# Moving a conditional block from the last group of experts to the middle of the expert loop

## The chip, the cores and the metric

The kernel runs on one core of a Trainium2 chip. The core has five engines that run their own instruction streams: PE (TensorE, the matrix engine), DVE (VectorE), ACT (ScalarE), POOL (GpSimd) and SP (SyncE, which here issues nearly all the DMAs). The engines wait for one another through semaphores. The metric is the time of one execution on the device in microseconds; the median of three runs of the kernel before is 983.52 us (981.23 to 983.72).

## The reference

Two decoder layers act on a residual stream of 256 tokens by 1024 channels, in float32. A layer first mixes tokens (differential attention and sparse attention, then an output projection and a layer norm), and then works on channels. The change is in the second part:

```python
def hierarchical_moe(x, w_rg, b_rg, w_re, b_re, w_g, w_u, w_d):
    ...                      # top-1 of 4 groups, then top-2 of 8 experts in it: weights comb
    for g in range(N_GROUPS):
        hg = silu(einsum('nd,edf->nef', xt, w_g[g])) * einsum('nd,edf->nef', xt, w_u[g])
        y = y + einsum('nef,efd->nd', hg * comb[:, g, :, None], w_d[g])
    return y
...
ffn = hierarchical_moe(x, ...)
ple = sigmoid(x @ w_ple_gate[i]) * (p[i] @ w_ple[i])
x = layer_norm(ALPHA * x + ffn + ple, ln2_g[i], ln2_b[i])
```

There are 32 experts, each with gate, up and down matrices (1024x256, 1024x256, 256x1024), so that a layer reads 96 MB of expert weights. A token goes to two of them.

## The kernel before

**Tiling.** The 32 experts are ranked by how many tokens they have. The 12 with the most get 64 slots each, the other 20 get 32 slots. They are worked on in 11 groups of 128 rows: six groups of two experts with 64 rows each, and five of four experts with 32 rows. In the order of the loop (`gi` = 0 to 10) the groups gi = 0, 1, 2, 4, 6 and 8 are of two experts, and gi = 3, 5, 7, 9 and 10 of four. An expert's weights are six loads of 512 KB: four of gate and up, two of down. So a group of two brings 12 loads, a group of four 24.

**A group.** `slots_of` marks and gathers the tokens of a group (PE products with the 0/1 marks `gs`), `front` multiplies the gathered tokens with the gate and up weights and applies the activation (`sil`), and `back` turns `sil` around (line 95, two transposes), copies it to `hT` (line 1058, ACT), multiplies it with the down weights, splits the product in two parts (lines 208 and 209, ACT and DVE) and adds them up into the four accumulators `acc` (`combine`). In the columns of PE's array each expert of a group has its own strip, of 64 or 32 columns; a 128x512 product of 32 columns is written `128*32 128x512` in the rows. Nearly all products go through one helper, line 92. The loop runs ahead by one: `front(gi + 1)` is issued before `back(gi)`.

**The block.** Some expert could have more tokens than slots. Then `rest` (line 1078 and around) works through what is left over, in two loops over experts (lines 1196 and 1198). The whole stands under `tc.If(most > 0)` (line 1195), where `most` is read from a small tensor `cmi` (line 1194) into a register of each engine. In the profiled execution `most` is zero in both layers: the block is jumped over, and the loops never run. On SP the way that skips the block ends in nine semaphore instructions (rows at line 1195), which bring the semaphores of SP's DMAs to the counts that the block would have left.

**Other work in the loop.** At gi = 4, 5 and 6 the pieces of the per-layer embedding (`Embed`, products of `x` and `p` with 256 columns) are worked in. At gi = 9 the two vectors of the layer norm are loaded (`wide`, line 382). At the last group of the first layer four weights of the next layer are loaded ahead (`ahead`, line 164).

**What sets the order.** A scheduler orders each engine's instructions from the program's order and its own estimates; a conditional is a border that it keeps: what the program has after the block is issued after it, with exceptions that the order below shows. Weights live in 47 places of 512 KB (`Held`). A load (`fetch`: line 1032 reads the expert's number, line 1038 issues the DMA; `load`: line 164) needs a free place, and so waits until PE has made the last product with what was there. All weight loads go through SP's one queue, in order: a load that waits holds all behind it. Eight semaphores are used in turn, so that at most eight loads are under way.

Of the kernel before, what the change touches and what calls it, by code (L numbers as in the profile page):

```python
# [23 lines left out]
DEPTH = 2  # L24
# [55 lines left out]

@with_exitstack
def tile_hybrid_trunk(ctx: ExitStack, tc: tile.TileContext, x_in, xT_in, pT_in, pos_in, ws, wik, wrt, lnv,
                      brt, lamv, sublnv, out, places=47, t2b=4, young=4, gsb=1, hTb=1, silb=2, nring=5, early=(4, 5, 6), nahead=4, apart=8, npre=36, wA=1, wB=1, wC=1, wD=1, wE=3, inorder=2, e0=3, e1=3,  nearly_=0, peng_=1, ifat=10, im=0, df=0, dh=15, nol=0, diag=1, rpool='0000', lastemb=1, lastat=6, pre_if=(4,5), npair=6, fh=False, fg=0, order=(0,1,2,6,3,7,4,8,5,9,10), engs=None, nemb=1, nwarm=9, nfine=2, nah=4, o1=False, o2=False, o3=True, o4=True, order2=True, pa=2, pb=7, f1=True):
    nc = tc.nc
    V, A, G = nc.vector, nc.scalar, nc.gpsimd

# [37 lines left out]
    def bank():  # L124
        return ps.tile([P, 512], F32, tag="mm", bufs=4, name=nm("mm"))

    def wt(shape, dt, tag, bufs):
        return wk.tile(shape, dt, tag=tag, bufs=bufs, name=nm(tag))
# [3 lines left out]
    class Held:  # L132
# [11 lines left out]
        def free(self):  # L144
            arena.give(self.b)
# [16 lines left out]
    def load(l, i, shape):  # L162
        r = Held(shape, load=True)
        nc.sync.dma_start(r.t, ws[l, i])
        return r
# [56 lines left out]
    ahead, ready = [], []  # L222
# [156 lines left out]
    def wide(i, l):  # L379

        r = Held([D])
        nc.sync.dma_start(r.v[0:1], lnv[l, i:i + 1])
        G.partition_broadcast(r.v, r.v[0:1])  # L383
        return r
# [68 lines left out]
    for l in range(DEPTH):  # L453
# [3 lines left out]
        ahead, ready = [], []  # L457
# [420 lines left out]
        groups = [[(r, 2, 64)] for r in range(0, 2 * npair, 2)]  # L878
# [9 lines left out]
        if order:  # L888
            groups = [groups[i] for i in order]

        def experts(gi):

            c = 0
            for r, n, w in groups[gi]:
                for i in range(n):
                    yield r + i, slice(c, c + w)
                    c += w

        def gather(gs, xg, halves=(0, 1)):

            for k4 in halves:
                b = bank()
                for k in range(4):
                    ks = slice((4 * k4 + k) * P, (4 * k4 + k + 1) * P)
                    for t in range(TT):
                        PE.matmul(b[:, k * P:(k + 1) * P], x[t].v[:, ks], gs[:, t, :], start=t == 0, stop=t == TT - 1)
                A.activation(xg.half[k4], b.rearrange("p (k s) -> p k s", k=4), AF.Copy)  # L907
# [17 lines left out]
        def marks_of(gi):  # L925

            gs = wt([P, TT, P], F32, "gs", gsb)
            c = 0
            for r, n, w in groups[gi]:
                marked[0] = V.tensor_tensor(gs[:, :, c:c + n * w].rearrange("p t (e s) -> p t e s", e=n),  # L930
                                            iom[:, None, None, :w].to_broadcast([P, TT, n, w]),
                                            posm[:, :, r:r + n, None].to_broadcast([P, TT, n, w]), op=OP.is_equal)
                c += n * w
            return gs

        def ways_of(gi, gs):

            sT = wt([P, TT, P], F32R, "sT", 2)
            bw = ways(gs, [cw[:, :, r:r + n] for r, n, w in groups[gi]], sT)
            wsl = wt([P, 1], F32, "wsl", 3)  # L940
            for i, (r, sl) in enumerate(experts(gi)):
                V.tensor_copy(wsl[sl], bw[sl, i:i + 1])
            return sT, wsl

        def slots_of(gi):
            gs, xg = marks_of(gi), Gathered(gi >= fg)
            gather(gs, xg)
            return xg, *ways_of(gi, gs)

        b = bank()  # L950
        places = bank()
# [61 lines left out]
        def between():  # L1013
            with in_turn():
                gather(gs, first, (1,))
            with in_turn():
                for t in range(TT):
                    PE.matmul(b[:, t * NE:(t + 1) * NE], combT[:, t * P:(t + 1) * P], perm, start=True, stop=True)
            with in_turn():
                r = ways_of(0, gs)  # L1020
            ranked = el4.rearrange("p t g e -> p t (g e)")
            V.tensor_copy(ranked, b[:, :2 * NE].rearrange("p (t e) -> p t e", t=TT))
            V.tensor_scalar(mks, ranked, 0.0, None, op0=OP.is_gt)
            V.tensor_copy(cw[:, :, NFIX:], ranked[:, :, NFIX:])
            return r
# [3 lines left out]
        def fetch(r, j):  # L1029

            if r >= NFIX and r not in ranks:
                ranks[r] = nc.sync.value_load(ids[0:1, r:r + 1], min_val=0, max_val=NE - 1)
            fetched[r, j] = Held([2, 512], load=True)
            if r < NFIX:
                src = ws[l, O_EXP + 6 * r + j]
            else:
                src = ws[l, ds(O_EXP + 6 * ranks[r] + j, 1)].rearrange("o p n -> (o p) n")
            nc.sync.dma_start(fetched[r, j].t, src)

        def weights_of(gi, js):  # L1040
            for j in js:
                for r, _ in experts(gi):
                    if (r, j) not in fetched:
                        fetch(r, j)
            return [[fetched.pop((r, j)) for r, _ in experts(gi)] for j in js]

        def hidden_act(gu, wsl, sil):
            A.activation(sil, gu[:, :FE], AF.Sigmoid)  # L1048
            V.scalar_tensor_tensor(sil, sil, wsl, gu[:, :FE], op0=OP.mult, op1=OP.mult)  # L1049
            V.tensor_tensor(sil, sil, gu[:, FE:], op=OP.mult)  # L1050
            return sil
# [71 lines left out]
        def front(gi, xg, sT, wsl, between=None):  # L1123

            sl = [sl for _, sl in experts(gi)]
            n = len(sl)
            wr = weights_of(gi, range(4))
            gu = bank()
            for kt in range(KT):
                for i in range(n):  # L1130
                    PE.matmul(gu[sl[i], :], xg.half[kt // 4][:, kt % 4, sl[i]],
                              wr[kt // 2][i].v[:, kt % 2, :], start=kt == 0, stop=kt == KT - 1)
                if kt % 2:
                    free(*wr[kt // 2])
                if kt == KT // 2 - 1 and between:
                    sT, wsl = between()
            xg.free()
            return hidden_act(gu, wsl, wt([P, FE], F32, "sil", silb)), sT
# [35 lines left out]
        for gi in range(len(groups)):  # L1174
            if gi == e1:
                emb[0].products(0, range(wE, KT + 2))
                emb[0].gate()
                emb[0].add(0)
            if gi == e0:
                emb[0].run(1)  # L1180
            if gi in early:
                q = 1 + early.index(gi)
                if q not in emb:
                    emb[q] = Embed(q)
                emb[q].run(0)
                if q < 3:
                    emb[q].run(1)
            if gi == ifat:
                for j in pre_if:
                    for r, _ in experts(gi):  # L1190
                        fetch(r, j)
                if l < DEPTH - 1:
                    ahead.extend(load(l + 1, i, [2, 512]) for i in range(nah))
                most = nc.values_load(cmi[0:1, 0:1], min_val=0, max_val=S)
                with tc.If(most > 0):
                    with tc.For_i(0, NBIG, 1) as r:
                        rest(r, 64, 2)
                    with tc.For_i(NBIG, NE, 1) as r:
                        rest(r, 32, 1)
            after = front(gi + 1, *slots_of(gi + 1)) if gi + 1 < len(groups) else None  # L1200
            if gi == lastat and (l == DEPTH - 1 or lastemb == 2):
                emb[3].run(1)
            ys, sT = back(gi, *held), held[1]
            held = after
            if gi == last - 1:
                lng, lnb = wide(2, l), wide(3, l)
                xn = [Held([D]) for _ in range(TT)]
                if l < DEPTH - 1:
                    xT = Split(KT)
# [102 lines left out]
```

## Time and profile before

| | |
|---|---|
| median of three runs | 983.52 us (981.23 to 983.72) |
| profiled execution, its own time | 980.9 us |
| its span in the trace | 978.8 us |
| mean granted clock of TensorE | 0.988 |
| PE busy | 936.4 us, 96% |
| DVE, ACT, POOL busy | 425.9, 348.1, 33.5 us |
| moved by DMA | 280.81 MB, mean 287 GB/s |

The span is the time from the first to the last instruction that the profiler saw. "Busy" counts the time in which an engine executes, without its waits, branches and DMA issues. The two layers lie at 0 to some 480 us and 480 to 978 us; the expert loop takes about the second half of each.

### The profile page before, as it was taken

What the parts mean: (1) busy time and instruction counts of PE and PEld (TensorE: products, weight loads), DVE (VectorE), ACT (ScalarE), POOL (GpSimd) and SP (SyncE); (2) the same over time, 40 slices, a digit from 0 to 9 for tenths busy, and PEclk for the clock granted to TensorE, in tenths of its full rate; (3) what the DMA queues carried; (4) which work ended last, traced back from release to release, by engine and by line L of the source; (5) the groups of instructions that cost most, each with busy time, mean ns of one, the idle gap of its engine ahead of it and who ended that gap; (6) DMA issues with size and microseconds to landing.
All of it is one profiled execution on the core that took longest, in us unless ns stands there. A gap on an engine that the chain in (4) does not pass through costs nothing. (4 is left out here: it accounts for less than half of the span.)

```text
span 978.8 us, 14760 instructions
## 1 busy us (share of the span) xinstructions
PE 936.4 (96%) x5185; PEld 608.9 (62%) x5185; DVE 425.9 (44%) x1066; ACT 348.1 (36%) x704; POOL 33.5 (3%) x36
## 2 busy tenths in 40 slices
PE   8999999999999999999699999999999999999983
PEld 5877777886445665444388767787754555664441
DVE  6796566863121121112468854768621211111113
ACT  6557586522111111111346667765111111111110
POOL 0000000100000000001310000001000000000010
PEclk9999999999999999999799999999999999999997
DMA  8994335777889999993899233466778899999823
GB/s 296 398 415 162 124 108 198 250 267 270 307 322 417 400 407 366 391 415 119 325 415 382 91 127 129 151 215 222 279 279 337 326 419 392 403 362 417 353 68 150
DMA packets 79010, 280.81 MB, mean 287 GB/s; under 512 B 9160, under 2 KB 9928, under 8 KB 78928
## 3 DMA queue, kind: packets, MB, share of 16 engines
q1 hardware_dynamic: 78784, 279.78, 75.2%
q8 instruction: 44, 0.72, 0.3%
q14 instruction: 38, 0.31, 0.1%
q10 hardware_dynamic: 144, 0.00, 0.0%
HBM read 278.70 MB, written 1.05 MB: 286 GB/s over the span
## 5 line engine op out<-in xcount | busy, mean ns | idle before, releaser
L92 PE MATMUL acc<-a,a 128*128 128x512 f32 x1440 | 352.2, 398 | 2.6 <-ACT a L208 1.8
L92 PEld LDWEIGHTS acc<-a,a 128*128 128x128 f32 x1440 | 266.0, 189 | 65.2 <-issue 3.2
L92 PE MATMUL mm<-a,a 128*32 128x512 f32 (+6 forms) x1456 | 240.7, 512 | 0.0
L208 ACT ACTIVATE a<-a 128x512 fp32r<-128x512 f32 (+1 forms) x247 | 150.7, 631 | 99.8 <-PE acc L92 66.5
L209 DVE TENSOR_TENSOR a<-a,a 128x512 fp32r<-128x512 f32 (+1 forms) x239 | 160.6, 692 | 51.5 <-ACT a L208 50.6
L92 PEld LDWEIGHTS mm<-a,a 128*32 128x32 f32 (+4 forms) x1456 | 111.7, 141 | 103.8 <-issue 94.8
L92 PE MATMUL mm<-a,hT 128*32 128x512 f32 (+1 forms) x512 | 113.5, 632 | 6.1 <-ACT hT L1058 5.9
L92 PEld LDWEIGHTS mm<-gs,a 128*128 128x128 f32 x704 | 85.5, 191 | 17.9 <-issue 13.5
L92 PE MATMUL mm<-gs,a 128*128 128x128 f32 x704 | 91.2, 278 | 0.0
L209 DVE TENSOR_TENSOR t<-mm,t 128x512 fp32r<-128x512 f32 x44 | 30.1, 691 | 137.1 <-ACT t L208 137.1
L1049 DVE SCALAR_TENSOR_TENSOR sil<-sil,wsl,mm 128x256 f32<-128x256 f32 x22 | 10.6, 480 | 131.5 <-ACT sil L1048 131.4
L208 ACT ACTIVATE t<-mm 128x512 fp32r<-128x512 f32 x44 | 26.0, 597 | 110.7 <-PE mm L92 109.6
L92 PE MATMUL acc<-t,sT 128*128 128x512 f32 x176 | 60.8, 441 | 2.9 <-ACT t L208 2.9
L92 PEld LDWEIGHTS mm<-a,hT 128*32 128x32 f32 (+1 forms) x512 | 26.9, 123 | 58.8 <-issue 41.9
L1048 ACT ACTIVATE sil<-mm 128x256 f32<-128x256 f32 x22 | 8.5, 384 | 140.2 <-PE mm L92 140.2
L92 PEld LDWEIGHTS acc<-t,sT 128*128 128x128 f32 x176 | 28.5, 189 | 33.8 <-ACT t L208 17.4
L907 ACT ACTIVATE a<-mm 128x512 f32<-128x512 f32 x40 | 23.9, 597 | 66.8 <-PE mm L92 66.7
L920 DVE CAST sT<-mm 128x256 fp32r<-128x256 f32 x22 | 9.3, 425 | 61.2 <-PE mm L92 58.6
L763 DVE TENSOR_TENSOR sil<-sil,mm 128x256 f32<-128x256 f32 x16 | 6.7, 420 | 53.5 <-ACT sil L762 53.5
L548 ACT ACTIVATE t<-mm,mx 128x128 f32<-128x128 f32 (+1 forms) x64 | 26.1, 422 | 10.7 <-DVE mx L545 10.7
L383 POOL PARTITION_BROADCAST a<-a x8 | 10.3, 1314 | 543.4 <-DMA a<-lnv 540.5
L762 ACT ACTIVATE sil<-mm 128x256 f32<-128x256 f32 x16 | 6.1, 384 | 57.9 <-PE mm L92 53.7
(195 smaller groups left out, 649.9 us busy)
## 6 DMA issues: line engine op xcount, KB each, us to landing
a<-ws SPq DMA_DIRECT2D x523, 512.0 KB, 8.6
a<-x_in SPq DMA_DIRECT2D x2, 512.0 KB
out<-a SPq DMA_DIRECT2D x4, 256.0 KB, 2.6
a<-xT_in SPq DMA_DIRECT2D x3, 256.0 KB, 5.6
a<-wik SPq DMA_DIRECT2D x2, 288.0 KB, 8.3
a<-ws SPq DMA_DIRECT2D x2, 256.0 KB, 4.2
pT<-pT_in SPq DMA_DIRECT2D x2, 256.0 KB, 9.3
a<-wrt SPq DMA_DIRECT2D x2, 144.0 KB, 2.5
```

The source lines that it names most:

```text
L92: self.last = nc.tensor.matmul(*a, **k)
L208: copied[0] = A.activation(hi, src, AF.Copy)
L209: copied[1] = eng.tensor_tensor(lo, src, hi, op=OP.subtract)
L383: G.partition_broadcast(r.v, r.v[0:1])
L548: A.activation(e[:, i * nk:(i + 1) * nk], b[:, i * nk:(i + 1) * nk], AF.Exp, bias=mx[:, i:i + 1], accum_out=sums[i])
L762: A.activation(g, b[:, :256], AF.Sigmoid)
L763: V.tensor_tensor(g, g, b[:, 256:], op=OP.mult)
L907: A.activation(xg.half[k4], b.rearrange("p (k s) -> p k s", k=4), AF.Copy)
L920: V.tensor_copy(sT, b[:, :2 * P].rearrange("p (t q) -> p t q", t=TT))
L1048: A.activation(sil, gu[:, :FE], AF.Sigmoid)
L1049: V.scalar_tensor_tensor(sil, sil, wsl, gu[:, :FE], op0=OP.mult, op1=OP.mult)
```

## The change

The condition moves from `gi == 10` to `gi == 3` (the default of `ifat`), and in the loop body from ahead of `front(gi + 1)` to behind it. So the block now stands behind the products of `front(4)`, the fifth group, and ahead of `back(3)`. The early loads of the last group's down weights (`pre_if`) and of the next layer's weights, which stood ahead of the block, go; `back(10)` issues both itself. The reading of `most` stays ahead of `front`.

```diff
-    ... ifat=10, ...
+    ... ifat=3, ...
             if gi == ifat:
-                for j in pre_if:
-                    for r, _ in experts(gi):
-                        fetch(r, j)
-                if l < DEPTH - 1:
-                    ahead.extend(load(l + 1, i, [2, 512]) for i in range(nah))
                 most = nc.values_load(cmi[0:1, 0:1], min_val=0, max_val=S)
+            after = front(gi + 1, *slots_of(gi + 1)) if gi + 1 < len(groups) else None
+            if gi == ifat:
                 with tc.If(most > 0):
                     with tc.For_i(0, NBIG, 1) as r:
                         rest(r, 64, 2)
                     with tc.For_i(NBIG, NE, 1) as r:
                         rest(r, 32, 1)
-            after = front(gi + 1, *slots_of(gi + 1)) if gi + 1 < len(groups) else None
```

Lines behind the change stand four lower afterwards, and the conditional itself at line 1192.

In SP's queue, first layer, this stood before around the new place (a_2803 is the last gate and up load of group gi = 4; a_2826 to a_2840 are the eight down loads of gi = 3; a_2963 to a_3020 the gate and up loads of gi = 5; a_3059 to a_3065 the down loads of gi = 4; L164 with a_3098 to a_3102 the weights of an `Embed`):

```order
L1038 DMA a_2803<-ws 128x1024
L1038 ISA
L1038 DMA a_2826<-ws 128x1024
...
L1038 DMA a_2840<-ws 128x1024
L1032 TENSOR_LOAD ids_2224
L1032 ISA x2
L1038 ISA
L1038 DMA a_2963<-ws 128x1024
...
L1038 DMA a_3065<-ws 128x1024
L164 DMA a_3098<-ws 128x1024
L164 DMA a_3100<-ws 128x1024
L164 DMA a_3102<-ws 128x1024
```

And this stands there now (a_2817 is the last gate and up load of gi = 4, the left-out rows are 19 more readings of line 1032; a_3416 to a_3420 are the same three `Embed` weights as a_3098 to a_3102, and a_3144 is the first down load of gi = 3):

```order
L1038 DMA a_2817<-ws 128x1024
L1032 TENSOR_LOAD ids_2224
L1032 ISA x2
...
L164 DMA a_3416<-ws 128x1024
L164 DMA a_3418<-ws 128x1024
L164 DMA a_3420<-ws 128x1024
L1192 COMPARE_AND_BRANCH
...
L1192 UNCONDITIONAL_BRANCH
L1038 ISA
L1038 DMA a_3144<-ws 128x1024
```

The 28 loads a_2826 to a_3065 moved from ahead of the three `Embed` loads to behind the block, and twenty readings of expert numbers moved ahead of it. Behind the block SP has 126 loads of 512 KB before it comes to the layer norm's vectors at line 382. The three `Embed` loads wait for the same products of PE as they did: the last one for the `128*128 128x256` products of `Embed` that end at about 301.7 us.

On PE, first layer, this stood before behind the products of `front(4)` (mm_2805; mm_2842 is the transposes of `back(3)`, and mm_2847 its down products, in the strips of the four experts, a_2826 to a_2840 being their weights):

```order
L92 MATMUL mm_2805<-a_2803,a_2740 64x512
L95 MATMUL mm_2842<-identr,sil_2669 128x128 x2
L92 MATMUL mm_2847<-a_2826,hT_2845 32x512
L92 MATMUL mm_2847<-a_2828,hT_2845 32x512
L92 MATMUL mm_2847<-a_2830,hT_2845 32x512
L92 MATMUL mm_2847<-a_2832,hT_2845 32x512
L92 MATMUL mm_2847<-a_2834,hT_2845 32x512
L92 MATMUL mm_2847<-a_2836,hT_2845 32x512
```

And this stands there now (mm_3165 and mm_3182 are the two halves of the same down product; mm_3199 is a product of `Embed` over all 128 columns, whose inputs have been there since before):

```order
L1192 UNCONDITIONAL_BRANCH
L95 MATMUL mm_3160<-identr,sil_2669 128x128 x2
L92 MATMUL mm_3165<-a_3144,hT_3163 32x512
L92 MATMUL mm_3182<-a_3144,hT_3163 32x512
L92 MATMUL mm_3165<-a_3146,hT_3163 32x512
L92 MATMUL mm_3182<-a_3146,hT_3163 32x512
L92 MATMUL mm_3199<-a_2308,a_2069 128x256 x4
L92 MATMUL mm_3165<-a_3148,hT_3163 32x512
L92 MATMUL mm_3182<-a_3148,hT_3163 32x512
L92 MATMUL mm_3199<-a_2310,a_2070 128x256 x3
L92 MATMUL mm_3165<-a_3150,hT_3163 32x512
L92 MATMUL mm_3182<-a_3150,hT_3163 32x512
```

Before, eight products of one half stood in a row, with four different strips next to one another. Now the two halves of one weight, in one strip, stand together, and products over all columns stand between them; the other four weights follow in the same manner.

## Rows read from the trace of the kernel before

**Rows 1.** Waits of the tensor engine, whole span: total us, times, longest
```profile
PE mm L95 <- PEq L1195: 13.7, 2, 7.3
PE mm L92 <- ACT hT L1058: 5.9, 11, 0.8
```

**Rows 2.** Timeline, TensorE, end of first layer: start, us, idle before
```profile
462.34 2.16 PE L92 MATMUL acc<-t,sT 128*128 128x512 f32 x8 [0.70 <-ACT t L208]
470.93 0.66 PE L95 MATMUL mm<-identr,sil 128*128 128x128 f32 x2 [6.43 <-PEq L1195]
472.40 6.75 PE L92 MATMUL mm<-a,hT 128*32 128x512 f32 x32 [0.81 <-ACT hT L1058]
```

**Rows 3.** Line 1195, first layer: ns (min, median, max), first and last start
```profile
L1195 SPq EVENT_SEMAPHORE  x9: 17/17/17, 471.2 to 480.7; - x9
...
L1195 PEldq COMPARE_BRANCH  x1: 6359/6359/6359, 464.3 to 464.3; - x1
```

**Rows 4.** Line 1195, second layer
```profile
L1195 PEldq COMPARE_BRANCH  x1: 7379/7379/7379, 951.1 to 951.1; - x1
```

**Rows 5.** Waits of SP's queue, first layer, 436 to 462
```profile
SPq L382 <- PE mm L92: 18.1, 1, 18.1
```

**Rows 6.** The same, second layer, 915 to 948
```profile
SPq L382 <- PE mm L92: 22.9, 1, 22.9
```

**Rows 7.** Line 1038, last down loads, first layer
```profile
L1038 SPq DMA_DIRECT2D a<-ws x8: 333/368/447, 460.8 to 464.7; - x8
...
DMA to landing us min/median/max: 4.6/6.9/8.1
```

**Rows 8.** The same, second layer
```profile
L1038 SPq DMA_DIRECT2D a<-ws x8: 332/369/662, 947.8 to 952.1; - x8
...
DMA to landing us min/median/max: 3.3/5.7/7.3
```

**Rows 9.** Timeline, TensorE, end of second layer
```profile
959.97 5.55 PE L92 MATMUL mm<-a,hT 128*32 128x512 f32 x32 [0.53 <-ACT hT L1058]
```

**Rows 10.** Timeline of SP's queue around the new place, first layer
```profile
265.12 38.14 SPq L1038 DMA_DIRECT2D a<-ws  x31
304.09 2.81 SPq L164 DMA_DIRECT2D a<-ws  x3
```

**Rows 11.** The same, second layer
```profile
786.83 2.81 SPq L164 DMA_DIRECT2D a<-ws  x3
```

**Rows 12.** Line 1032, reads of an expert's number on SP, whole span
```profile
L1032 SPq TENSOR_LOAD <-ids x52: 262/268/461, 227.9 to 891.7; - x52
```

**Rows 13.** Timeline, TensorE, around the new place, first layer
```profile
298.96 2.75 PE L92 MATMUL mm<-a,a 128*128 128x256 f32 x12
307.07 7.09 PE L92 MATMUL mm<-a,a 128*64 128x512 f32 x32
315.00 2.76 PE L92 MATMUL mm<-a,hT 128*32 128x512 f32 x18 [0.47 <-ACT hT L1058]
...
318.37 1.06 PE L92 MATMUL mm<-a,hT 128*32 128x512 f32 x8
...
320.03 1.06 PE L92 MATMUL mm<-a,hT 128*32 128x512 f32 x6
...
335.84 7.07 PE L92 MATMUL mm<-a,a 128*32 128x512 f32 x64
...
348.81 1.07 PE L92 MATMUL mm<-a,hT 128*64 128x512 f32 x2
```

**Rows 14.** Stretches: us, busy of PE, PEld, DVE, ACT, POOL; PEclk, DMA share, GB/s
```profile
321.00:400.00 79.00, 77.55 (x475) 46.95 (x472) 14.22 (x37) 13.20 (x28) 0.00 (x0) 1.00 0.97 385
400.00:438.00 38.00, 37.15 (x217) 18.00 (x220) 6.01 (x16) 5.22 (x10) 0.00 (x0) 1.00 1.03 416
438.00:460.00 22.00, 22.00 (x166) 10.47 (x162) 4.13 (x11) 3.33 (x7) 0.00 (x0) 1.00 0.32 131
...
470.90:479.50 8.60, 7.76 (x36) 2.65 (x37) 0.69 (x1) 1.76 (x4) 1.21 (x1) 0.60 0.94 375
```

More of the change, by code (lines that the diff above doesn't have):

```diff
@@ L82, in tile_hybrid_trunk @@
 def tile_hybrid_trunk(ctx: ExitStack, tc: tile.TileContext, x_in, xT_in, pT_in, pos_in, ws, wik, wrt, lnv,
-                      brt, lamv, sublnv, out, places=47, t2b=4, young=4, gsb=1, hTb=1, silb=2, nring=5, early=(4, 5, 6), nahead=4, apart=8, npre=36, wA=1, wB=1, wC=1, wD=1, wE=3, inorder=2, e0=3, e1=3,  nearly_=0, peng_=1, ifat=10, im=0, df=0, dh=15, nol=0, diag=1, rpool='0000', lastemb=1, lastat=6, pre_if=(4,5), npair=6, fh=False, fg=0, order=(0,1,2,6,3,7,4,8,5,9,10), engs=None, nemb=1, nwarm=9, nfine=2, nah=4, o1=False, o2=False, o3=True, o4=True, order2=True, pa=2, pb=7, f1=True):
+                      brt, lamv, sublnv, out, places=47, t2b=4, young=4, gsb=1, hTb=1, silb=2, nring=5, early=(4, 5, 6), nahead=4, apart=8, npre=36, wA=1, wB=1, wC=1, wD=1, wE=3, inorder=2, e0=3, e1=3,  nearly_=0, peng_=1, ifat=3, im=0, df=0, dh=15, nol=0, diag=1, rpool='0000', lastemb=1, lastat=6, pre_if=(4,5), npair=6, fh=False, fg=0, order=(0,1,2,6,3,7,4,8,5,9,10), engs=None, nemb=1, nwarm=9, nfine=2, nah=4, o1=False, o2=False, o3=True, o4=True, order2=True, pa=2, pb=7, f1=True):
     nc = tc.nc
```

## The prediction

> **What bounds the kernel now.** I read the waits of the tensor engine first. Over the whole span only one wait of PE is large: 13.7 us in two pieces, both at the conditional block; the next cause, copies by ACT, adds up to 5.9 us in 11 pieces of at most 0.8 [rows 1]. No DMA is among its waits. So PE is the bound, and its one gap is what the change moves. Then I looked at where the gap lies. In the first layer PE ends the additions of group 9 at 464.50 (462.34 + 2.16), stands 6.43 us, and does the 32 down products of the last group from 472.40 to 479.15 [rows 2]. The gap is the branch itself: the instruction takes 6.36 us on PE in the first layer [rows 3] and 7.38 in the second [rows 4].
>
> Third, what else was late in that place. SP's queue stood 18.1 us (to 459.96) in the first and 22.9 us (to 946.95) in the second layer, at the layer norm's vectors, waiting for a place that PE had to release [rows 5, 6]; the last group's eight down loads stand behind it. They were issued up to 464.7 and 952.1, and the slowest landed 8.1 and 7.3 us later [rows 7, 8], so by about 472.8 and 959.4. PE's products began 0.4 before the one and 0.6 after the other [rows 2, 9]. So at the end the branch lies beside a transfer that PE would have waited for anyway. That is the first thing to see: the gap is 13.7 us, but what can be won by taking it away is less.
>
> Fourth, the new place. There SP is well ahead of PE. It issues the loads of line 1038 without a break until 303.3, and then the three Embed loads, at 304.09 to 306.90 [rows 10] and from 786.83 in the second layer [rows 11].
>
> **The change part by part.**
>
> *The end.* Without the branch, PE can end the last down products no sooner than the last weight's landing, and what is left then: one weight's two halves in one strip. A piece of two matmuls of this kind takes 1.07 [rows 13], two pieces in a strip some 1.9 (2 x 1.07 less 0.2 that they share, an estimate from these rows). So 474.7 instead of 479.15, and 961.3 instead of 965.52 (959.97 + 5.55): at most 4.4 and 4.2 us. [...] I take 2 per layer, the middle. The early loads that were removed from ahead of the block cost nothing, since these loads keep their place behind line 382.
>
> *PE's branch in the middle.* It stands behind the 32 products of front(4), 7.09 us [rows 13]. Its price has no row in the middle. From above it is 7.38 us [rows 4]. From below it is 0: PE's queue may run ahead of its products, and the branch may be taken while they still run. At the end it could not, because the last additions waited for ACT, and so the branch began at 464.3, 0.2 before they ended [rows 2, 3]. I take 5 us, nearer to the two rows that exist.
>
> [...]
>
> *PE's order behind the block.* Before, back(3) makes its 32 products in pieces of 18, 8 and 6, in 2.76 + 1.06 + 1.06 = 4.9 us [rows 13]: four strips run side by side. Behind the block the two halves of one weight stand together, in one strip, and full-width Embed products between them. The order makes six turns of the eight weights (two of them have two weights side by side, four have one). A turn is 4 matmuls in a strip, some 1.9 us as above; six are 11.4, 6.5 more than before. From above: eight turns, 15.2, so 10.3 more. From below: 0, if the turns overlapped fully. That a piece costs the same however little is in it, the rows show: 8 matmuls take 1.06 and 6 take 1.06, but 2 also take 1.07.
>
> So PE comes out of the middle 5 + 6.5 = 11.5 us later in each layer.
>
> *SP's queue.* The block makes SP wait until all of its loads under way have landed: at the end the nine semaphore instructions began at 471.2 and the last at 480.7 [rows 3]. In the middle it comes to the branch behind the three Embed loads, and the last of these waits for PE's Embed products, which end at 301.71 (298.96 + 2.75) [rows 13]. The 20 readings of expert numbers ahead of it, 0.27 us each and 5.4 in all [rows 12], lie within that wait. From 301.8 on: the last Embed load lands 3.3 us after issue, as into an empty queue [rows 8], so at 305.1; some 0.5 for the semaphores; the first down load lands at 305.6 + 3.3 = 308.9. Its own eight follow at 1.26 us each (524288 bytes at 416 GB/s [rows 14]), the last at 317.7. PE's first down product stands at 315.0 plus the branch; it is hardly held. The next 16, for front(5), have landed by 338, and PE, which began these at 335.84 [rows 13] and now 11.5 later, isn't held either.
>
> But 28 loads are now behind the block that had been issued by 304: some 35 us of transfer. What stood in SP at line 382 is the slack for it. 126 loads lie between the block and line 382. At 1.28 us (between 1.26 and the 1.36 of the 385 GB/s stretch [rows 14]) the last lands at 308.9 + 125 x 1.28 = 468.9, where SP was released at 459.96 before: 8.9 late. In the second layer all this lies 481.8 later (its L164 loads, at 786.83, 482.7), so 790.7 + 160 = 950.7 against 946.95: 3.8 late. Both are under PE's own 11.5, so PE's lateness sets the release, and the stream is beside it. At 1.26 they would be 6.4 and 1.3, at 1.36 18.9 and 13.8 late.
>
> *The sum.* Per layer 5 + 6.5 - 2 = 9.5, for two layers 19. The profiled execution took 980.9 us (span 978.8); 19 more are 999.9. The median of the runs is 2.6 above it, so I predict 983.5 + 19 = 1002.5 us.
>
> **The rivals.**
>
> *The middle covers it, and it gets faster.* If the branch is taken while the products of front(4) run, and the turns overlap, then the middle costs nothing and the end gives 4.4 + 4.2: 983.5 - 8.6 = 974.9. For it: the weights for the next products lie ready, and SP had 18 to 23 us of slack. Against it: 35 us of loads are put off, more than the slack, and the order puts turns of one strip between full-width products. It decides where the middle costs under 2.8 us a layer (4.3 less half of 3). Chance 0.07.
>
> *Loss and gain are equal.* One of the two terms on PE is small and the end gives its most: some 4.3 lost and 4.3 won per layer, 983.5. For it: each term has 0 as an end. Against: the stream is 6.4 late in the first layer even at 1.26. Chance 0.07.
>
> *The branch hides, the order doesn't.* The sequencer gets ahead of PE by the 7.09 us of front(4), none of whose products has to wait. Then 2 x (6.5 - 2) = 9 more: 992.5. For it: in 0.2 us ahead of a chain that waits for ACT there is no proof of more or less. Against: a branch of 7 us needs a lead of 7 us. Chance 0.15.
>
> [...]
>
> *The stream becomes the bound.* With 1.36 us a load, PE waits for weights up to the end: 18.9 + 13.8 = 32.7, and no gain at the end since its loads come as late: 1016.2. For it: the stretch of 385 GB/s. Against: the next stretch reaches 416 GB/s, and no row says that the DMA, not a wait for places, held the slower one. Chance 0.16.
>
> **How the numbers follow.** The forecast has 0.55. A measurement of this kernel tells some 0.3% (3 us) from no change. Faster has 0.07; the same 0.07 and a tail of the cheap branch, so 0.08; the rest, 0.85, is slower. The range goes from the cheap branch with a gain of 3 at the end (983.5 + 7 = 990.5) up to both terms of PE at their upper ends (2 x (7.4 + 10.3) = 35.4 without any gain: 1018.9): 990 to 1019.
>
> **What would show it.** In the profile after: PE's gap at the conditional in the middle of each layer (some 5 us behind front(4)) and none at the end; at the end, waits of PE for DMA at the last down products; back(3)'s down products spread over 11 to 12 us with 256-column products between; SP's queue with no issue from about 279 to 305 but the Embed loads; the DMA slices around 280 to 305 near empty; SP's wait at line 382 shorter by more than half in the first layer. It would be wrong if PE showed no gap and no spread there, if weights came so late that PE waits for DMA throughout 340 to 460, or if the end were shorter by far more than 4 us.

## The result and the profile after

The changed kernel takes 1010.79 us (median; 1008.01 to 1013.74, 4 runs), and the kernel before, timed beside it, 983.33 (981.23 to 983.72). The ratio is 1.0284, with a 95% interval of 1.0255 to 1.0313: 27.5 us slower. I had forecast 1002.5 within 990 to 1019. The direction and the main place were right; the sum, 19, was 8 short.

The profiled execution after has a span of 1005.7 us, 26.9 more than before. Where they came in is read from one recurring row of TensorE's timeline: the four small products `mm<-cw,gs` that stand just ahead of the `front` of each group. Their start times:

| place | before | after | later by |
|---|---|---|---|
| layer 1, group 4 | 306.64 | 305.61 | -1.0 |
| layer 1, group 5 | 335.41 | 346.17 | 10.8 |
| layer 1, group 10 | 449.34 | 458.46 | 9.1 |
| layer 2, group 0 | 717.01 | 729.36 | 12.4 |
| layer 2, group 4 | 788.46 | 800.84 | 12.4 |
| layer 2, group 5 | 817.22 | 838.85 | 21.6 |
| layer 2, group 7 | 869.98 | 890.22 | 20.2 |
| layer 2, group 8 | 895.52 | 919.63 | 24.1 |
| layer 2, group 10 | 936.33 | 961.93 | 25.6 |
| end of the span | 978.8 | 1005.7 | 26.9 |

The stretch with the moved block (group 4 to 5) got 11.8 and 9.2 us longer; then 1.6 are regained in the first layer and 4.0 more lost in the second; and the end of a layer, where the block was taken away, is 3.2 and 1.3 us longer, not shorter (in the first layer this stretch also holds the next layer's token mixing).

What kind of time it is, the page of the kernel after tells (engine busy; then groups of products: busy, mean ns | idle before); the last two lines are the same groups before:

```profile
PE 968.0 (96%) x5185; PEld 615.3 (61%) x5185; DVE 425.7 (42%) x1066; ACT 347.5 (35%) x704; POOL 33.3 (3%) x36
...
L92 PE MATMUL mm<-a,a 128*32 128x512 f32 (+6 forms) x1456 | 251.8, 514 | 0.0
...
L92 PE MATMUL mm<-a,hT 128*32 128x512 f32 (+1 forms) x512 | 133.1, 604 | 2.9 <-ACT hT L1058 2.0
```

```profile
L92 PE MATMUL mm<-a,a 128*32 128x512 f32 (+6 forms) x1456 | 240.7, 512 | 0.0
L92 PE MATMUL mm<-a,hT 128*32 128x512 f32 (+1 forms) x512 | 113.5, 632 | 6.1 <-ACT hT L1058 5.9
```

PE is busy 31.6 us longer (936.4 before) with the same 5185 products: the down products `mm<-a,hT` take 19.6 more (113.5 before), the group `mm<-a,a` 11.1 more (240.7 before). The mean granted clock is no lower (0.991, before 0.988). So the loss is hardly idle time. The waits of PE say the same (total, times, longest):

```profile
PE mm L95 <- DVE a L414: 4.9, 2, 4.2
PE mm L95 <- PEq L1192: 2.5, 1, 2.5
PE mm L95 <- DVEq L1192: 2.4, 1, 2.4
...
PE mm L92 <- DMA a<-ws: 0.7, 1, 0.7
```

The 13.7 us of [rows 1] are gone, 4.9 have come at the new place, and PE waits 0.7 us for weights in the whole span. The two at the new place differ: in the first layer PE waits for DVE to pass the block, in the second for its own branch. The timeline of PE around the new place, first layer, answers to [rows 13]:

```profile
306.05 7.09 PE L92 MATMUL mm<-a,a 128*64 128x512 f32 x32
315.52 0.30 PE L95 MATMUL mm<-identr,sil 128*128 128x128 f32 x1 [2.38 <-DVEq L1192]
316.64 0.27 PE L95 MATMUL mm<-identr,sil 128*128 128x128 f32 x1 [0.82 <-issue]
317.44 2.66 PE L92 MATMUL mm<-a,hT 128*32 128x512 f32 x8 [0.53 <-ACT hT L1058]
320.03 2.90 PE L92 MATMUL mm<-a,a 128*128 128x256 f32 x8
322.86 1.90 PE L92 MATMUL mm<-a,hT 128*32 128x512 f32 x4
324.69 1.56 PE L92 MATMUL mm<-a,a 128*128 128x256 f32 x6
326.19 1.90 PE L92 MATMUL mm<-a,hT 128*32 128x512 f32 x4
```

The six turns are there (pieces of 8, 4, 4, 8, 4, 4), a turn of four products takes 1.90, as worked out, and Embed products stand between. The six turns add up to 12.2 us here and 11.5 in the second layer, where the same products took 4.9 in both before. With the Embed products between them they spread over 21 us. SP's queue, first layer, answers to [rows 10], and its wait at line 382 to [rows 5] and [rows 6]:

```profile
295.87 5.18 SPq L164 DMA_DIRECT2D a<-ws  x3
306.00 49.87 SPq L1038 DMA_DIRECT2D a<-ws  x44
356.71 1.68 SPq L164 DMA_DIRECT2D a<-ws  x2
359.38 100.24 SPq L1038 DMA_DIRECT2D a<-ws  x80
```

```profile
SPq L382 <- PE mm L92: 7.1, 1, 7.1
...
SPq L382 <- PE mm L92: 15.8, 1, 15.8
```

The first load behind the block is issued at 306.00 (forecast: some 305.6). SP still stands at line 382 for 7.1 us in the first and 15.8 in the second layer: the stream of weights had time left in both.

Last, the ends of the layers. The first layer, answering to [rows 2]:

```profile
475.89 2.75 PE L92 MATMUL mm<-a,hT 128*32 128x512 f32 x8
478.58 1.99 PE L92 MATMUL mm<-a,a 128*128 128x256 f32 x8
480.50 1.90 PE L92 MATMUL mm<-a,hT 128*32 128x512 f32 x4
...
489.90 1.82 PE L92 MATMUL acc<-t,sT 128*128 128x512 f32 x6 [0.81 <-ACT t L208]
495.97 1.09 PE L95 MATMUL mm<-identr,a 128*128 128x128 f32 x4 [4.24 <-DVE a L414]
```

No branch stands there any more, but the down products of the last group now also alternate with Embed products, and these are used up when the layer norm comes (DVE, line 414): PE stands 4.24 us. The second layer, answering to [rows 9], has no Embed products left:

```profile
979.37 10.36 PE L92 MATMUL mm<-a,hT 128*32 128x512 f32 x28
990.41 1.90 PE L92 MATMUL mm<-a,hT 128*32 128x512 f32 x4 [0.68 <-DMA a<-ws]
```

The eight last down weights are issued from 975.5 to 979.4, up to the moment at which PE begins with them. Before, they were issued from 947.8 to 952.1 [rows 8] and PE began at 959.97. The 32 products now take 12.95 us from first to last, where they took 5.55 [rows 9].

### The profile page after: what moved, and what is told of

The parts are those of the page before. It is cut to its first block, busy times and chain, and to the rows that moved or that the text cites. A ratio compares the mean times of both kernels' runs of the same rounds, so it can differ in the third digit from the quotient of the medians.

```text
span 1005.7 us, 14711 instructions
## 1 busy us (share of the span) xinstructions
PE 968.0 (96%) x5185; PEld 615.3 (61%) x5185; DVE 425.7 (42%) x1066; ACT 347.5 (35%) x704; POOL 33.3 (3%) x36
## 5 line engine op out<-in xcount | busy, mean ns | idle before, releaser
L92 PE MATMUL mm<-a,a 128*32 128x512 f32 (+6 forms) x1456 | 251.8, 514 | 0.0
L92 PE MATMUL mm<-a,hT 128*32 128x512 f32 (+1 forms) x512 | 133.1, 604 | 2.9 <-ACT hT L1058 2.0
L92 PEld LDWEIGHTS mm<-a,hT 128*32 128x32 f32 (+1 forms) x512 | 30.9, 119 | 71.5 <-issue 57.9
L208 ACT ACTIVATE t<-mm 128x512 fp32r<-128x512 f32 x44 | 25.6, 597 | 120.5 <-PE mm L92 120.5
L92 PE MATMUL acc<-t,sT 128*128 128x512 f32 x176 | 54.3, 427 | 5.4 <-ACT t L208 5.3
```

The lines of the kernel that those rows point to most:

```text
L92: self.last = nc.tensor.matmul(*a, **k)
L208: copied[0] = A.activation(hi, src, AF.Copy)
```

## The experiments

All ratios are to the kernel before, timed beside them, with a 95% interval. "O" is the theory that PE's order costs, "S" that late weights cost, "B" that the branch itself costs.

**1. The order alone.** Down products are held in the order of the program.

```diff
                     for i in range(n):
-                        PE.matmul(yp[sl[i], :], hT[:, f, sl[i]], ...)
+                        with in_turn() if (h or f or i) else ExitStack():
+                            PE.matmul(yp[sl[i], :], hT[:, f, sl[i]], ...)
```

> The changed kernel, with the down products of every group's back() held in the order of the program (half, then row block, then expert), so that products of different strips stand side by side again; the loads stay behind the block. Theory O (order): most of the 27.5 us is PE's own order, the late loads are beside it. Then the time falls by 13 to 18 us, to 993 to 998, and PE still waits for no weights worth speaking of. Theory S (stream): the weights come late after the block, and PE's drawn-out order only fills the time until they land. Then PE now shows waits for DMA in the place of the Embed products between, and the time falls by less than 5, to above 1006. Theory B (the branch itself, paid anew at 5 to 7 us a layer): no more than 3 us, above 1008.

Measured: 1.0198 (1.0162 to 1.0234), 1000.58 us. Between the two: a good 8 us regained, less than O wanted. PE now has waits for weights and for copies:

```profile
PE acc L92 <- ACT t L208: 14.7, 21, 0.8
PE mm L92 <- DMA a<-ws: 5.7, 12, 1.4
```

These waits are not what is left of the loss. Experiment 3 holds the same order with the loads ahead, has nearly the same waits, and is 15.5 us faster:

```profile
PE acc L92 <- ACT t L208: 14.2, 20, 0.8
PE mm L92 <- DMA a<-ws: 4.6, 8, 1.3
```

From 300 to 450 us, where the 28 loads are late, PE waits for no weights in either run. So the row of waits doesn't bear out theory S. By the stretches of the table above, experiment 1 is longer than experiment 3 by 2.7 and 2.5 us in the stretch with the block, by 3.9 at the end of the first layer, and by 4.9 in the second layer from group 7 to 8. In the stretch with the block, PE in the first layer works at a lower granted clock behind its gap (0.50; in experiment 3 0.71), and in the second it stands 3.8 us for its branch, where experiment 3 stands 1.8 for DVE. The 4.9 are order again, but of products that this edit doesn't hold: Embed products stand between the group's gate and up products, and these 64 take 11.4 us, in the changed kernel too, where they took 7.1 before (first the changed kernel, then before):

```profile
L92 PE MATMUL mm<-a,a 128*32 128x512 f32 x64 | 11.4, 598 | 0.0
```

```profile
L92 PE MATMUL mm<-a,a 128*32 128x512 f32 x64 | 7.1, 594 | 0.0
```

**2. Loads ahead.** The 28 loads are issued ahead of the block, as before.

```diff
             if gi == ifat:
+                for g, js in ((gi, (4, 5)), (gi + 2, range(4)), (gi + 1, (4, 5))):
+                    for j in js:
+                        for r, _ in experts(g):
+                            if (r, j) not in fetched:
+                                fetch(r, j)
                 with tc.If(most > 0):
```

> The changed kernel, with 28 loads (the down weights of group 3, the gate and up weights of group 5, the down weights of group 4) issued ahead of the block as the kernel before has them there. The scheduler then orders back(3) as in the kernel before, in runs of four strips. Theory O with the order following from where the loads stand: 990 to 995, all of the lost order regained and the branch of some 3 us a layer still paid. Theory S: the same loads are on time, so also about 990 to 995; what tells the two apart is the run with the order alone. Theory B: stays above 1005, since the branch is as it was.

Measured: 1.0048 (1.0033 to 1.0062), 985.56 us. Some 23 of the 27.5 us come back, with the block where the change put it; more than the 990 to 995 that I expected. The scheduler again orders back(3) in runs of four strips, unforced:

```profile
306.26 7.09 PE L92 MATMUL mm<-a,a 128*64 128x512 f32 x32
315.73 0.57 PE L95 MATMUL mm<-identr,sil 128*128 128x128 f32 x2 [2.38 <-DVEq L1197]
316.83 4.46 PE L92 MATMUL mm<-a,hT 128*32 128x512 f32 x18 [0.53 <-ACT hT L1058]
```

Here the stretch from group 4 to 5 shows the block's own price, the order being that of [rows 13]: 4.3 us more than before in the first and 2.5 in the second layer. In the first it is 2.38 idle, 0.2 for the rest of the chain, and 1.7 because the next 18 products take 4.46 instead of 2.76 at a granted clock of 0.61:

```profile
313.40:316.80 3.40, 0.57 (x2) 0.20 (x2) 1.33 (x3) 0.77 (x2) 0.00 (x0) 1.00 0.71 216
316.80:321.20 4.40, 4.37 (x18) 0.86 (x18) 0.69 (x1) 0.60 (x1) 0.00 (x0) 0.61 0.98 304
```

**3. Both together** (the two edits above).

> Both of the others: loads ahead of the block and down products in program order. Theory O: as the better of the two and some 4 less, since groups 7 to 10 get their strips too: 983 to 989. Theory S: as with the loads ahead, 990 to 995. Theory B: above 1003.

Measured: 1.0035 (1.0018 to 1.0051), 985.03 us: as with the loads ahead alone. Once the loads are ahead, forcing the order adds nothing that can be told, and costs nothing either.

**4. No block.** The reading of `most` and the conditional are taken out of the changed kernel.

> Leaves out the conditional and its reading (tokens beyond the slots would be lost; there are none here). It gives the price of the block as a whole. If the block in the kernel before cost its 13.7 us of idle time, this takes about 970; if, as I predicted, most of that lay beside the last group's late down weights, 979 to 984 (at most 4.4 us a layer under the kernel before). Against the changed kernel: theories O and S some 27 less, theory B about 14 less.

Measured: 1.0027 (1.001 to 1.0043), 984.48 us. It is not faster than the kernel before, though that stands 13.7 us in its branches. Taking the block away wins nothing there by itself. Its profile has the end of the changed kernel: last down products between Embed products, and 4.25 us of waiting for the norm.

**5. Eight of the 28 loads ahead** (the edit of experiment 2 with `((gi, (4, 5)),)` alone).

> The changed kernel with only the eight down loads of group 3 ahead of the block; the other 20 loads stay behind it. The scheduler then orders back(3) in runs of four strips, as before. Theory O3 (the lost order in group 3 is what costs, 7.5 and 6.7 us as between the changed kernel and the one with 28 loads ahead): some 14 us less than the changed kernel, a ratio to before of about 1.013. Theory S (20 loads are still late, and later groups pay for it in PE's order or in waits): less than 7 us regained, a ratio above 1.021. All regained (ratio under 1.008) would say that the other 20 loads don't matter at all.

Measured: 1.0174 (1.0146 to 1.0201), 999.9 us: some 11 regained, between the two. The stretch from group 4 to 5 falls to 5.15 us more than before in each layer; but the loss in groups 7 to 9 of the second layer and at the ends stays. So the 20 other loads cost about as much as the eight, and mostly not in group 3.

**6. The kernel before, with its last weights on time.** Line 382 held SP since its vectors got a place that had just been freed; now they get the one free longest.

```diff
     def wide(i, l):
-        r = Held([D])
+        r = Held([D], load=True)
```

> The kernel before with one thing changed: the two layer norm vectors of line 382 take the place that has been free longest, so that SP isn't held there and the last group's down weights are on time; the block stays at the end. My account of the end (branch and late weights lie side by side, and either alone would cost as much): the time stays within 0.5% of the kernel before, PE's gap at line 1195 stays at 6 to 7 us a layer. The other account (the late weights were what cost, the branch is hidden): 5 to 10 us faster.

Measured: 0.9943 (0.9922 to 0.9965), 975.84 us. 5.6 us faster than before, with the block at the old place. The size is that of the other account, but neither had the way: PE's gap was not kept but halved (6.6 us in two), because the branch itself got shorter (3.34 and 3.30 us, before 6.36 and 7.38):

```profile
469.76 0.66 PE L95 MATMUL mm<-identr,sil 128*128 128x128 f32 x2 [3.40 <-PEq L1195]
471.23 5.56 PE L92 MATMUL mm<-a,hT 128*32 128x512 f32 x32 [0.81 <-ACT hT L1058]
```

**7. No block, and the same places.**

> Leaves out the conditional (tokens beyond the slots would be lost; there are none here), and has the same places for the layer norm vectors. My account of the end: with both covers gone the time falls by 5 to 10 us under the kernel without the block alone, to a ratio to before of 0.992 to 0.998. If the branch cost nothing at the end and the late weights neither: unchanged at 1.003.

Measured: 0.9948 (0.9928 to 0.9967), 975.86 us. 7 to 8 us under experiment 4, as my account had it, but equal to experiment 6, which has the block. So late last weights did cost; the branch at the end, once the weights are on time, doesn't show against the order that its border gives.

**8. Loads ahead, and the same places** (the edits of experiments 2 and 6 on the changed kernel).

> The changed kernel with the 28 loads ahead of the block, and the same places for the layer norm vectors: a version that may beat both. My account: 5 to 8 us less than with the loads ahead alone (1.0048), so 0.997 to 1.000. If the end is bound by something else (the order of the last products and the layer norm behind them): unchanged at 1.004 to 1.005.

Measured: 0.9959 (0.9943 to 0.9974), 978.02 us: faster than both kernels, and under experiment 2 by a little more than my account gave. Nearly all of that lies at the end of the second layer (7.8 us): its eight last loads are issued from 929.0 where experiment 2 has 951.7, and the 32 products take 3.68 us where they take 12.42 there.

**9. And the Embed products back behind the last group.**

```diff
             if t == 0 and l < DEPTH - 1 and lastemb < 2:
-                emb[3].products(1)
+                with in_turn():
+                    emb[3].products(1, range(0, 1))
+                emb[3].products(1, range(1, KT + 2))
```

> The changed kernel with 28 loads ahead of the block and the layer norm vectors in the place longest free, as in the run before (0.9959), and the first layer's last Embed products (128x256) held behind the additions of the last group, where the kernel before has them, instead of between its down products. My account of the end of the first layer (the order there, and a layer norm that no product covers, cost some 3 us): 3 to 6 us less than that run, a ratio of 0.990 to 0.993. If the wait for the norm stays as long whatever PE does before it: unchanged at 0.996.

Measured: 0.9853 (0.9835 to 0.9872), 967.8 us: 14 us under the kernel before and 43 under the changed one. It is 10 us under experiment 8, well beyond the 3 to 6 that I expected. The end of its first layer:

```profile
466.07 3.68 PE L92 MATMUL mm<-a,hT 128*32 128x512 f32 x32
470.54 1.82 PE L92 MATMUL acc<-t,sT 128*128 128x512 f32 x6 [0.79 <-ACT t L208]
472.19 3.61 PE L92 MATMUL mm<-a,a 128*128 128x256 f32 x16
...
476.61 0.63 PE L95 MATMUL mm<-identr,a 128*128 128x128 f32 x4
```

The 32 down products take 3.68 us where they took 6.75 [rows 2], and the Embed products lie under the layer norm: the next layer's group 0 stands at 710.5, 6.5 before that of the kernel before. Its end in the second layer is 7 us shorter than before too; that comes with experiment 8, where it is as short.

**10. The same without the block.**

> Leaves out the conditional (tokens beyond the slots would be lost; there are none here); otherwise the same two changes as in the run beside it. What is left of the block's price in the middle of the loop: 3 to 4 us a layer by the middle stretches so far, so a ratio some 0.006 to 0.008 under the run beside it, 0.983 to 0.987. If the block's border also helps the order elsewhere, the two are alike within 0.003.

Measured: 0.9859 (0.9838 to 0.988), 967.95 us: alike. Without the block the stretch from group 4 to 5 is 3.9 and 3.5 us shorter, but the stretch from group 7 to 10 is longer, by 3.4 and 3.6; the second of the two expectations.

**11. The changed code, block at the last group** (`ifat=10`).

> The changed kernel's code with the condition left at the last group: the block stands at the old place, and the last group's down weights and the next layer's four weights are fetched behind it, as the changed code has it. If loads behind the block are what costs wherever it stands: slower than before by 6 to 14 us (1.006 to 1.014), PE waiting for the last down weights. If the early loads that the change removed cost nothing, as I predicted for the moved block: within 0.3% of before.

Measured: 1.011 (1.0091 to 1.013), 993.39 us. The early loads that the change removes are worth 11 us where the block stands at the end. In the trace nearly all of it lies at the end of the first layer (14.5 us more from its group 10 to the next layer's group 0, against 1.4 at the end of the second); this is the slowest of the four runs, 3.6 above their median. The edit takes away the down weights and the next layer's four weights together, and no run parts the two. PE waits for weights, and the order falls apart as in the middle:

```profile
468.43 0.66 PE L95 MATMUL mm<-identr,sil 128*128 128x128 f32 x2 [3.72 <-PEq L1192]
...
474.29 4.24 PE L92 MATMUL mm<-a,hT 128*32 128x512 f32 x10 [2.47 <-DMA a<-ws]
478.46 1.13 PE L92 MATMUL mm<-a,a 128*128 128x256 f32 x4
```

**12. The changed kernel with the edit of experiment 9 alone.**

> The changed kernel with only the first layer's last Embed products held behind the last group's additions. If the order at the end of the first layer costs 3 us there too: 2 to 5 us less than the changed kernel, a ratio of 1.023 to 1.026. If the last down weights come so late that PE has the time anyway: unchanged at 1.028.

Measured: 1.029 (1.027 to 1.0311), 1010.64 us: nothing. With its last weights late, PE now waits and drags there instead:

```profile
479.48 10.66 PE L92 MATMUL mm<-a,hT 128*32 128x512 f32 x28 [0.95 <-DMA a<-ws]
```

So the order at the end pays only together with the weights on time: experiments 8 and 9 differ by 10 us, the changed kernel and experiment 12 by none.

## Why the prediction was right, and where it was short

**The order behind the block: right, in size too.** I put it at 6.5 us a layer, six turns of 1.9 for 4.9. The six turns measure 12.2 and 11.5 us, so 7.3 and 6.6 more. Between the changed kernel and the one with 28 loads ahead the stretch from group 4 to 5 differs by 7.5 and 6.7 us. Only my sign for it, a spread of 11 to 12 us, forgot the Embed products between.

**The branch: the size near, the way wrong.** I took 5 us of PE standing in its branch, with 0 and 7.4 as ends. The stretches of experiment 2 give 4.3 and 2.5. But PE's branch there begins at 309.56, under products of front(4) that run to 313.35, and takes 2.85 us: it is hidden, as the rival had it. What shows is that PE's first product behind the block waits for DVE to pass the block too, and DVE has to finish front(4)'s activation first (in the changed kernel at 314.56; it has passed the block at 315.4, and PE starts at 315.52). Then comes the lower clock behind the idle stretch (0.61). In the second layer of the changed kernel both ways end together: PE's branch takes 6.13 us, from 804.38 under products that run to 808.37, and is over at 810.5, DVE has passed at 810.3, and PE stands 2.46 us. So of the 5 us that I took about half shows as a gap of PE, 2.4 and 2.5. The rival that the branch hides and costs nothing (992.5) fell with that.

**The end: the step that failed.** I took a gain of 2 us a layer, at most 4.4, at least 0. No run shows the 2, nor the 0 below it, which were estimates of mine: the stretches there are 3.2 and 1.3 us longer. I had asked when the last weight lands by the times of the kernel before, and left the order of the last group's products as it was. In the second layer the last weights come late now, and their products take 12.95 us instead of 5.55 (with the loads on time 3.68, experiment 8); that uses up the 7.28 us that PE had stood in the branch. In the first layer it is the order: in the kernel before, the block was also a border that kept Embed products behind the down products; they covered the layer norm. Without it the scheduler spends them between the down products, and the norm lies open. The cost of that is also the clock behind the gap: the kernel is 9.1 us late at group 10, 10.9 at the transposes behind the norm, and 12.6 at the next ones, at 505.62. (The last three numbers of a row are the granted clock, the DMA share and GB/s; first the kernel after, then the matching stretch before, which begins with the same transposes.)

```profile
495.90:503.00 7.10, 6.41 (x20) 5.21 (x21) 6.34 (x11) 1.61 (x3) 6.28 (x6) 0.52 1.03 422
```

```profile
485.00:492.00 7.00, 6.15 (x31) 5.03 (x32) 6.92 (x12) 1.60 (x4) 6.96 (x6) 1.00 1.01 395
```

"The early loads that were removed cost nothing" belongs to this step, and is its first fault: they keep their place behind line 382, but PE, which no longer stands in a branch, comes to them sooner. Experiment 11 shows 11 us for them at the old place; at the new place it wasn't tried alone, but experiment 8 gains some 9 over experiment 2 by having the last group's loads on time.

**Left out of the sum: the other groups.** I took PE's order to change in group 3 alone. In the second layer the stretch from group 7 to 8 takes 3.9 us longer; experiment 2 has none of that, experiment 5 all of it. It is the Embed products between the strips of a group's gate and up products (experiment 1). So with the 20 loads behind the block the order changes far behind it. That the scheduler's estimate of their arrival does this is argued from the runs; the estimates themselves were not looked at.

**The stream: right that it isn't the bound, wrong that it is beside the matter.** PE waited 0.7 us for weights, and SP kept slack at line 382, so the rival with the stream as the bound (1016.2) fell. But with the loads ahead some 23 of 27.5 us are gone. What the traces show of the way is mostly order: the turns behind the block (7.3 and 6.6 us) and the gate and up products from group 7 to 8 (4.3). I read the order as given and did not ask what made it; whoever asks sees that the 28 loads that SP had behind the block and the six turns on PE are one thing. Holding the down products' order with the loads still behind the block regains about a third (experiment 1, 1.0198). What stays there is not paid in waits for weights near the block, since PE has none, but in the pieces named at that experiment; about 1.5 of its 15.5 us to experiment 3 stay without a place.

**The sum.** Forecast 2 x (5 + 6.5 - 2) = 19. Measured 11.8 + 9.2 in the middle (forecast 23), 3.2 + 1.3 at the ends (forecast -4), 2.4 in the groups between (forecast 0), and 1.0 less ahead of it: 26.9.

## What to carry to other kernels

The conditional divided the program here though its body never ran: what was issued behind it came later, and the scheduler gave the other engines another order with it. Put the loads that the next groups need ahead of it, and compare each engine's order over the whole stretch, not only at the border. A busy time that grows with the same number of instructions at the same clock can be a loss of order, as here (31.6 us more for the same 5185 products, at a granted clock of 0.991, before 0.988), and the list of waits didn't show it. An idle gap is worth only what is ready behind it: leaving out the block gave nothing in any of three runs (experiment 4 against the kernel before, 7 against 6, 10 against 9). What paid was to have the last weights on time and the layer norm covered. And before a wait is called the price of an order, look for the same wait in a run that has the order and not the loss.

## What the hardware showed that I had not expected

PE's branch past the block had no fixed price in these runs. With the DMA engines nearly idle it took 3.34 and 3.30 us (experiment 6), with them full 6.36 and 7.38 (the kernel before). The stretches of the branch itself (the last three numbers are the granted clock, the DMA share and GB/s), in the kernel before and in experiment 6:

```profile
464.26:470.62 6.36, 0.24 (x2) 0.00 (x0) 0.00 (x0) 0.00 (x0) 0.00 (x0) 0.75 1.02 343
951.08:958.46 7.38, 0.42 (x2) 0.00 (x0) 0.00 (x0) 0.00 (x0) 0.00 (x0) 0.80 0.96 342
```

```profile
466.10:469.44 3.34, 0.25 (x2) 0.00 (x0) 0.00 (x0) 0.00 (x0) 0.00 (x0) 0.83 0.09 30
949.68:952.98 3.30, 0.38 (x2) 0.00 (x0) 0.00 (x0) 0.00 (x0) 0.00 (x0) 1.00 0.03 7
```

In the second layer of the changed kernel and of experiments 1, 5 and 12 it took 6.13, 7.47, 7.13 and 6.37 us at DMA shares of 0.95 to 1.01, in experiment 2 2.85 and 3.55 at 0.37 and 0.39. But the price doesn't follow the share alone. In the first layer of those four it took only 0.77 to 1.86 us at 0.77 to 0.97, and in the second layer of experiment 11 4.48 at 0.90.

What it goes with stands in the same traces. The profile lists a queue q8 of the kind "instruction": 44 packets with 0.72 MB in the kernel before, 45 with 0.74 in the changed one, each of 16384 bytes. In all 22 branches of the eleven traces that have the block, PE's branch ends 2.3 to 2.7 us after such a packet starts (2.33 and 2.37 in the kernel before, 2.46 and 2.36 in the changed one). What varies is when the packet comes: 1.0 us after the branch's start in experiment 6, 4.0 and 5.0 in the kernel before, 3.8 to 5.1 in the four slow branches of the second layer, and 0.5 to 1.6 us ahead of the branch in the four short ones of the first layer. Three of them in stretches of 0.2 us (packets, MB, share of 16 engines): the kernel before at 468.2, experiment 6 at 467.02, and the changed kernel at 308.42, ahead of its branch at 309.35:

```profile
q8 instruction: 1, 0.02, 30.2%
```

```profile
q8 instruction: 1, 0.02, 30.0%
```

```profile
q8 instruction: 1, 0.02, 34.1%
```

So the branch ended at about the same distance behind the packet each time, and it was short (0.77 to 1.86 us) where the packet had started ahead of it. That the branch waits for what the packet brings is my reading of these times; no run moves the packet alone. Why the packet comes later in some of the branches is not shown either: it came 4.0 and 5.0 us after the branch's start at DMA shares of 1.02 and 0.96, but 1.8 us after it in the second layer of experiment 11, at 0.90.
